# A gated three-branch encoder layer on one core: the last branch's gate blocks four to seven as two Strassen block products

## The chip, the core and the metric

The kernel runs on one core of a Trainium2 chip. TensorE (PE, its weight loads PEld) multiplies, VectorE (DVE), ScalarE (ACT) and GpSimd (POOL) do the elementwise work, SyncE (SP) issues most transfers. The metric is the time of one execution in microseconds (us) of device time. The three runs of the kernel before took 917.25 to 917.41 us, their median is 917.26 us.

## The reference, cut to what matters

One layer for 512 tokens of width 1024. Three branches (A sparse attention, B stick-breaking attention, C attention into memory tokens) are projected up, each multiplied by a sigmoid gate of its own that is computed from the normalised input, and summed; then come an output projection, a norm, and a SwiGLU feed-forward network (FFN).

```
h = rmsnorm(x, g_mix_pre[l])
proj = h @ w_in[l]
aq, ak, av, iq, ik, iw, bq, bk, bv, cq, gate_logits = jnp.split(proj, split_points, axis=-1)
...
ya = dsa_attention(aq, ak, av, iq, ik, iw, rel_bias) @ w_up_a[l]
yb = stick_breaking_attention(bq, bk, bv) @ w_up_b[l]
yc = memory_attention(cq, mk, mv) @ w_up_c[l]
gates = jax.nn.sigmoid((gate_logits + b_gate[l]).astype(jnp.float32)).astype(x.dtype)
gates = gates.reshape(bsz, seq, N_BRANCH, D_MODEL)
merged = gates[:, :, 0] * ya + gates[:, :, 1] * yb + gates[:, :, 2] * yc
x = x + rmsnorm(merged @ w_out[l], g_mix_post[l])
h = rmsnorm(x, g_ffn_pre[l])
gu = h @ w_ffn_in[l]
f = (jax.nn.silu(gu[..., :D_FF]) * gu[..., D_FF:]) @ w_ffn_out[l]
x = x + rmsnorm(f, g_ffn_post[l])
```

## The kernel before

**Precision.** Every float32 operand is split into a high part (a cast to fp32r on ACT) and a low part (the operand less its high part, on DVE). `split` does it, line 74 and line 75. Each block product is then three matmuls, `passes`, lines 85 to 87: high by high, high by low, low by high. So the third matmul of a product is the first that needs the low part of the weights.

**Tiling.** A block is 128 output columns for all 512 tokens. `feat` makes one block over `kc` slices of 128 inputs: a gate block has 8 slices and 24 matmuls of 512 columns, an up-projection block 4 slices and 12 matmuls.

**Merging a branch.** `merge(b, out, wu)` goes over eight blocks j. For each it makes gate block j + 1 (weights from `w_in`, the sum through a sigmoid, L693), the up-projection of block j (`wu` by the branch's output `out`), their product (L709, DVE) and the sum into `acc[j]` (L710, POOL). For branch B, the last one, `acc[j]` is split once more into `mT[j]`, the input of the output projection. Branch B's merge is queued while B's attention runs: its gate blocks 0 and 1 fill gaps of that attention, the rest comes after the attention's end.

**What follows.** `mix_out` (matmuls on L734) multiplies `mT` by `w_out`, adds the rows of `x` (`x1`, tiles `fin`) and norms. `ffn` makes the first three FFN blocks plainly and the other 19 with `seven`: a pair of blocks (gate half and up half) over two token halves is a 2 by 2 block product, and is made as seven products of 12 matmuls of 256 columns each (Strassen's scheme in Winograd's form), 84 matmuls in place of 96 of 256 columns (or 48 of 512). For that the activations have to be combined once (`right_sides`: eight additions on POOL, L828, eight subtractions on DVE, L832, four splits of 1024 columns) and the weights of each pair once (`left_sides`: four subtractions or additions on DVE, L860, three splits of 1024 columns and one of 512).

**Order and buffers.** PE's order is that of the code. On the other engines a scheduler of the compiler sets one fixed order per engine, and each engine works through it in that order. SBUF buffers are tiles of pools: the pool `att` holds the buffers of the attentions, the pool `late` (tags `lraw`, `fin`, `w2`, `s1` to `s3`) is opened after `att` is closed, in the same memory, so its first use waits until the last reader of `att` is done. That reader is the DVE split of branch B's last output (tile `vsum`, read at L75). `wraw`, `wh`, `wl` and `act` are tags of a pool that is open throughout.

Of the kernel before, what the change touches and what calls it, by code (L numbers as in the profile page):

```python
# [11 lines left out]
F32 = mybir.dt.float32  # L12
F32R = mybir.dt.float32r
AF = mybir.ActivationFunctionType
# [3 lines left out]
P = 128  # L18
# [29 lines left out]
class Layer:  # L48
# [212 lines left out]
    def run(self):  # L261
# [4 lines left out]
        with self.tc.manual_schedule(engines={mybir.EngineType.PE}):  # L266
# [412 lines left out]

    def merge(self, b, out, wu):  # L680

        nc, a = self.nc, self.a
        if b == 1:
            self.mT = []
        gates = {}

        def gate(j):
            c = C_G + b * D + j * P
            gw = self.weights(a["w_in"][:, c:c + P], NK, P)
            ps = self.bank()  # L690
            yield from self.feat(ps, gw, self.hT)
            gates[j] = self.sb.tile([P, T], F32, name="gate", tag="gate", bufs=2)
            nc.scalar.activation(gates[j], ps, AF.Sigmoid, bias=self.cols[:, 24 + b * 8 + j:25 + b * 8 + j])  # L693

        yield from gate(0)
        for j in range(NK):
            if j + 1 < NK:
                yield from gate(j + 1)
# [12 lines left out]
            if b == 1:  # L711
                self.mT.append(self.pair("act"))
                self.split(*self.mT[j], self.acc[j])
# [60 lines left out]
    def mix_out(self):  # L774
# [3 lines left out]
        self.x1 = [self.load_rows(a["x"], t, "fin") for t in range(NT)]  # L778
# [38 lines left out]
    def right_sides(self):  # L817

        nc, a, b = self.nc, slice(0, 256), slice(256, 512)
        y = {p: [tuple(x[:, t] for x in self.h2[f + k]) for k in range(4)]  # L820
             for p, f, t in ((1, 0, a), (2, 4, a), (3, 4, b))}
        y |= {p: [] for p in (4, 5, 6, 7)}
        for i in range(2):
            r = [self.big("act", F32).rearrange("p (k t) -> p k t", k=2) for _ in range(2)]
            for f in range(2):
                for k in range(2):
                    hi, lo = self.h2[4 * f + 2 * i + k]
# [12 lines left out]
    def left_sides(self, j):  # L840

        nc = self.nc
        g = self.load(self.a["w_ffn_in"][:, j * P:j * P + P], NK, P, "wraw")[0]
        u = self.load(self.a["w_ffn_in"][:, DFF + j * P:DFF + j * P + P], NK, P, "lraw")[0]
# [30 lines left out]
    def seven(self, j, y, f):  # L875

        nc, x = self.nc, self.left_sides(j)
        px, py, pz = (self.bank()[:, 0:256] for _ in range(3))
        s1, s2, s3 = (self.late.tile([P, 256], F32, name=n, tag=n, bufs=1 + (n == "s3")) for n in ("s1", "s2", "s3"))
        g = self.sb.tile([P, T], F32, name="silu", tag="gate", bufs=2)  # L880
# [6 lines left out]
        nc.vector.tensor_tensor(g[:, 0:256], py, s1, op=OP.add)  # L887
# [102 lines left out]
```

## Time and profile before

| what | value |
|---|---|
| median of 3 runs | 917.26 us |
| the profiled execution's own time | 917.32 us |
| its span, first to last instruction | 915.5 us |
| PE busy | 887.9 us, 97% of the span |
| DVE, ACT, POOL busy | 644.4, 457.6, 122.3 us |
| mean granted clock of TensorE | 0.995 of full speed |

The span is 1.8 us shorter than the execution's time; the difference lies before the first and after the last instruction. A row of a timeline gives start, duration, engine, line, operation and tiles; "x4" means that four instructions are merged in it; brackets give the engine's idle time before it and what ended that. Starts of one engine can lie closer than its durations, since instructions overlap a little.

### The profile page before, as it was taken

Reading aid. Unit: us, or ns where it says so; the run is one execution under the profiler, and the core shown is the slowest. Engines: PE = TensorE matmul, PEld = TensorE weight load, DVE = VectorE, ACT = ScalarE, POOL = GpSimd, SP = SyncE. Lnnn points to the kernel's source line nnn. Section 1 sums busy time; section 2 is a strip of 40 time slices with the busy share of each in tenths; the row PEclk is TensorE's granted clock in tenths of the full one; section 3 lists DMA queues with packets and bytes.
Section 4 is the critical chain, followed back from the end, with each engine's and each line's share of the span. In section 5 each row is a group of like instructions: output and inputs, shape, how many; then the busy total and the mean of one; then the engine's idle time right before and its main releaser. Section 6 shows DMA issues by size and latency. Waiting matters only on the chain.

```text
span 915.5 us, 13446 instructions
## 1 busy us (share of the span) xinstructions
PE 887.9 (97%) x5110; PEld 780.3 (85%) x5110; DVE 644.4 (70%) x1122; ACT 457.6 (50%) x804; POOL 122.3 (13%) x155
## 2 busy tenths in 40 slices
PE   5999999999999999999999999899999999999997
PEld 4889788888888888888788788899999999888885
DVE  7579999963588976777563478688888887932215
ACT  6365575332576666665353355355555555821111
POOL 4000000020032304443212123400000000000000
PEclk9999999999999999999999999899999999999999
DMA  6433543444354433222473524203334334533102
GB/s 213 127 93 116 175 125 93 127 119 112 103 150 127 127 82 92 69 59 58 136 252 107 184 83 125 69 28 112 107 102 116 97 112 131 168 93 100 38 0 92
DMA packets 129541, 101.17 MB, mean 111 GB/s; under 512 B 4652, under 2 KB 115292, under 8 KB 129476
## 3 DMA queue, kind: packets, MB, share of 16 engines
q1 hardware_dynamic: 128884, 99.26, 37.2%
q10 hardware_dynamic: 592, 1.05, 0.3%
q8 instruction: 40, 0.66, 0.3%
q14 instruction: 25, 0.20, 0.1%
HBM read 93.73 MB, written 2.12 MB: 105 GB/s over the span
## 4 chain that ended last, share of the span: by engine, by line
PE 82%; DVE 9%; issue 3%; ACT 2%; DMA 1%; POOL 1%; POOLq 0%; DVEq 0%; SPq 0%; ACTq 0%
PE bank L85 19%; PE bank L86 19%; PE bank L87 19%; PE bank L734 15%; DVE wl L75 3%; PE bank L534 2%; PE bank L549 1%; PE bank L179 1%; PE bank L178 1%; PE bank L209 1%; PE bank L211 1%; PE bank L210 1%; DMA lraw<-in_w_ffn_in_dram 1%; DVE e L621 1%; DVE score L506 1%
## 5 line engine op out<-in xcount | busy, mean ns | idle before, releaser
L75 DVE TENSOR_TENSOR wl<-wraw,wh 128x1024 fp32r<-128x1024 f32 (+1 forms) x112 | 130.6, 1167 | 100.4 <-ACT wh L74 100.1
L74 ACT CAST wh<-wraw 128x1024 fp32r<-128x1024 f32 (+1 forms) x112 | 107.3, 959 | 141.7 <-PE bank L86 79.5
L85 PE MATMUL bank<-h,wh 128*128 128x512 f32 (+1 forms) x376 | 148.8, 396 | 0.0
L87 PE MATMUL bank<-h,wl 128*128 128x512 f32 (+1 forms) x376 | 145.3, 386 | 1.0 <-DVE wl L75 0.9
L86 PE MATMUL bank<-h,wh 128*128 128x512 f32 (+1 forms) x376 | 145.0, 386 | 0.0
L734 PE MATMUL bank<-w,act 128*128 128x512 f32 x360 | 89.0, 393 | 0.0
L87 PEld LDWEIGHTS bank<-h,wl 128*128 128x128 f32 x376 | 70.6, 188 | 15.9 <-DVE wl L75 1.7
L85 PEld LDWEIGHTS bank<-h,wh 128*128 128x128 f32 x376 | 70.9, 189 | 11.7 <-PE bank L341 0.2
L86 PEld LDWEIGHTS bank<-h,wh 128*128 128x128 f32 x376 | 70.8, 188 | 11.4
L734 PEld LDWEIGHTS bank<-w,act 128*128 128x128 f32 x360 | 67.4, 188 | 15.0
L734 PE MATMUL bank<-wh,act 128*128 128x512 f32 x240 | 72.5, 393 | 0.0
L85 PE MATMUL bank<-act,wh 128*128 128x256 f32 (+1 forms) x204 | 69.2, 339 | 0.7 <-DVE s L896 0.7
L86 PE MATMUL bank<-act,wh 128*128 128x256 f32 (+1 forms) x204 | 67.9, 333 | 0.0
L87 PE MATMUL bank<-act,w 128*128 128x256 f32 x228 | 64.1, 281 | 0.0
L85 PE MATMUL bank<-h,w 128*128 128x256 f32 x228 | 64.1, 281 | 0.0
L86 PE MATMUL bank<-h,w 128*128 128x256 f32 x228 | 64.1, 281 | 0.0
L87 PE MATMUL bank<-h,w 128*128 128x256 f32 x228 | 64.1, 281 | 0.0
L85 PE MATMUL bank<-act,w 128*128 128x256 f32 x228 | 64.1, 281 | 0.0
L86 PE MATMUL bank<-act,w 128*128 128x256 f32 x228 | 64.1, 281 | 0.0
L241 POOL TENSOR_TENSOR rs<-ms,mhalf 128x1 f32<-128x1 f32 x18 | 12.1, 674 | 387.7 <-DVE ms L240 384.0
L598 POOL TENSOR_TENSOR p<-toep,score 128x128 f32<-128x128 f32 (+3 forms) x32 | 31.6, 1001 | 199.2 <-DVE score L507 103.0
L734 PEld LDWEIGHTS bank<-wh,act 128*128 128x128 f32 x240 | 45.0, 188 | 9.9
(189 smaller groups left out, 2113.3 us busy)
## 6 DMA issues: line engine op xcount, KB each, us to landing
wraw<-in_w_in_dram SPq DMA_DIRECT2D x64, 512.0 KB, 3.6
lraw<-in_w_ffn_in_dram SPq DMA_DIRECT2D x22, 512.0 KB, 3.9
wraw<-in_w_ffn_in_dram SPq DMA_DIRECT2D x22, 512.0 KB, 3.7
wraw<-in_w_ffn_out_dram SPq DMA_DIRECT2D x11, 512.0 KB, 3.6
lraw<-in_w_ffn_out_dram SPq DMA_DIRECT2D x11, 512.0 KB, 3.5
wraw<-in_w_mem_kv_dram SPq DMA_DIRECT2D x8, 512.0 KB, 3.7
lraw<-in_w_out_dram SPq DMA_DIRECT2D x6, 512.0 KB, 5.5
wraw<-in_w_out_dram SPq DMA_DIRECT2D x6, 512.0 KB, 3.7
```

The lines of the kernel that those rows point to most:

```text
L74: self.nc.scalar.copy(hi, src)
L75: (eng or self.nc.vector).tensor_tensor(lo, src, hi.bitcast(F32), op=OP.subtract)
L85: self.nc.tensor.matmul(out, lhsT=sh, rhs=mh, start=first and i == 0, stop=False, **kw)
L86: self.nc.tensor.matmul(out, lhsT=sh, rhs=ml, start=False, stop=False, **kw)
L87: self.nc.tensor.matmul(out, lhsT=sl, rhs=mh, start=False, stop=last and i == n - 1, **kw)
L178: self.nc.tensor.matmul(out, lhsT=x, rhs=y[:, 0:n], start=True, stop=False)
L179: self.nc.tensor.matmul(out, lhsT=x, rhs=y[:, T:T + n], start=False, stop=True)
L209: self.nc.tensor.matmul(ps, lhsT=ah[:, s], rhs=wh[:, k2], start=st, stop=False)
L241: self.nc.gpsimd.tensor_tensor(r, ms, self.mhalf, op=OP.pow)
L534: self.nc.tensor.transpose(ps[:, c:c + P], p[i][:, j * P:(j + 1) * P], self.ident)
L598: nc.gpsimd.tensor_tensor(s, toep[0][:, 0:n][:, ::-1], self.mask[i], op=OP.add)
L734: self.nc.tensor.matmul(ps[c], lhsT=st_[:, s], rhs=mv_[:, 0, c * 512:(c + 1) * 512], start=f and k == order[0], stop=l and k == order[-1])
```

## The change

Gate blocks 0 to 3 of branch B stay as they are; blocks 4, 5 and 6, 7 become two pairs that `seven` makes. For that `seven` is given its weights, its outputs and what to do with each sum (`glu` is the FFN's form of it), `right_sides` is called a second time, on the input `hT`, and the pool `late` is opened before branch B's merge, not after it. The up-projection's weights of branch B are split into tiles `fin` of the new pool, no longer into `wh` and `wl`. The rows of `x` (`x1`) are loaded some way into `mix_out`, since `fin` has other work before.

```
@@ run
-            self.outB = []
-            self.add(self.merge(1, self.outB, "w_up_b"))
+            self.outB, gates = [], {}
+            self.add(self.gates(1, (0, 1), gates))
             self.branch_b(*b)
-            self.drain()
             att.close()
             self.late = late.enter_context(self.tc.tile_pool(name="late", bufs=1))
+            ys = self.right_sides(self.hT)
+            self.drain()
+            self.add(self.merge_pairs(1, self.outB, "w_up_b", ys, gates))
+            self.drain()
             self.mix_out()
...
+    def merge_pairs(self, b, out, wu, ys, plain):
+        nc, a = self.nc, self.a
+        self.mT = []
+        gates = {}
+        def gate(i):
+            j = 2 * i
+            c = C_G + b * D + j * P
+            gates[i] = g = self.big("fin", F32)
...
+            yield from self.seven(
+                self.left_sides(a["w_in"], c, c + P), ys, g[:, q[0]], g[:, q[1]],
+                lambda: nc.scalar.activation(g[:, 0:512], g[:, 0:512], AF.Sigmoid, bias=bias[0]),
+                second, lambda px: nc.scalar.activation(g[:, q[2]], px, AF.Sigmoid, bias=bias[1]))
+        def up(j):
+            raw, _ = self.load(a[wu][:, j * P:(j + 1) * P], 4, P, "wraw")
+            t = self.big("fin")
+            w = [t[:, c:c + 512].rearrange("p (k c) -> p k c", c=P) for c in (0, 512)]
+            self.split(t[:, 0:512], t[:, 512:1024], raw)
+            y = self.bank()
+            yield from self.feat(y, w, out, kc=4)
...
+        first = 2
+        for j in range(2 * first - 1):
+            if j + 1 not in plain:
+                yield from self.gates(b, (j + 1,), plain)
+            yield from up(j)
+        prev = gate(first)
+        yield from step(prev, 4)
+        yield from up(2 * first - 1)
+        for i in range(first, NK // 2):
+            g = gate(i + 1) if 2 * i + 2 < NK else None
...
@@ mix_out
-        self.x1 = [self.load_rows(a["x"], t, "fin") for t in range(NT)]
+        self.x1 = []
...
+                if not self.x1 and us > 5:
+                    self.x1 = [self.load_rows(a["x"], t, "fin") for t in range(NT)]
@@ right_sides, left_sides, seven
-    def right_sides(self):
+    def right_sides(self, h):
-    def left_sides(self, j):
+    def left_sides(self, w, cg, cu):
-    def seven(self, j, y, f):
+    def seven(self, x, y, g0, g1, first, second, third):
```

PE's order after the attention's end is now: up-projection block 0, gate block 2, up 1, gate 3, up 2, six products of the first pair, up 3, two products of the second pair, the last of the first, up 4, three of the second, up 5, its last two, up 6, up 7.

Three other engines' orders at the attention's end. First DVE, from the last split that the attention itself needs. Before, where `vsum` is the last output of branch B, `act_4643` its low part, `wl_4669` the low part of up block 0's weights, `wl_4693` that of gate block 2's weights and `gate_4616` the product of block 0:

```order
L75 TENSOR_TENSOR wl_4669<-wraw_4666,wh_4668 128x512
L556 TENSOR_TENSOR vsum_4553<-bank_4631,vlow_4640 64x512
L75 TENSOR_TENSOR act_4643<-vsum_4553,act_4643 128x512
L75 TENSOR_TENSOR wl_4693<-wraw_4690,wh_4692 128x1024
L709 TENSOR_TENSOR gate_4616<-bank_4672,gate_4616 128x512
```

After, where `fin_4708` and `fin_4763` hold the weights of up blocks 0 and 1, `w2_4731` those of gate block 2, L895 is the subtraction of `right_sides` and `act_4667`, `act_4671` are low parts of its results:

```order
L75 TENSOR_TENSOR act_4643<-vsum_4553,act_4643 128x512
L895 TENSOR_TENSOR act_4656<-act_4656 128x2x256
L895 TENSOR_TENSOR act_4656<-act_4657,act_4656 128x2x256
L75 TENSOR_TENSOR fin_4708<-wraw_4706,fin_4708 128x512
L895 TENSOR_TENSOR act_4657<-act_4657,act_4656 128x2x256
L75 TENSOR_TENSOR fin_4763<-wraw_4761,fin_4763 128x512
L895 TENSOR_TENSOR act_4657<-act_4657 128x2x256
L75 TENSOR_TENSOR act_4667<-act_4656,act_4666 128x1024
L745 TENSOR_TENSOR gate_4616<-bank_4711,gate_4616 128x512
L75 TENSOR_TENSOR act_4671<-act_4657,act_4670 128x1024
L895 TENSOR_TENSOR act_4674<-act_4674 128x2x256
L75 TENSOR_TENSOR w2_4731<-lraw_4729,w2_4731 128x1024
```

The low part of up block 0's weights moved from ahead of `vsum` to behind two subtractions that follow it, and between `act_4643` and the low part of gate block 2's weights, neighbours before, stand ten instructions.

ACT at the same place, before, where `wh_4692` is the cast of gate block 2's weights and `gate_4664` the sigmoid of gate block 1:

```order
L74 CAST act_4643<-vsum_4553 128x512
L74 CAST wh_4692<-wraw_4690 128x1024
L693 ACTIVATE gate_4664<-bank_4624,cols_96 128x512
L74 CAST wh_4725<-wraw_4723 128x512
L74 CAST act_4687<-act_2069 128x512
```

And after, where `act_4666` and `act_4670` are casts of results of `right_sides`:

```order
L74 CAST act_4643<-vsum_4553 128x512
L74 CAST fin_4708<-wraw_4706 128x512
L74 CAST fin_4763<-wraw_4761 128x512
L74 CAST fin_4818<-wraw_4816 128x512
L74 CAST act_4666<-act_4656 128x1024
L691 ACTIVATE gate_4704<-bank_4624,cols_96 128x512
L74 CAST w2_4731<-lraw_4729 128x1024
L74 CAST act_4670<-act_4657 128x1024
```

The cast of gate block 2's weights has five instructions between itself and `act_4643`, and the second cast of `right_sides` stands behind it.

SP's queue, with the semaphores that each transfer waits for. Before, `wraw_4690` brings gate block 2's weights, and the first load into the pool `late` is `fin_5070`, a row block of `x`:

```order
L95 DMA wraw_4666<-in_w_up_b_dram 128x4x128 [waits DMAHW6_49,DVE_49]
L95 DMA wraw_4690<-in_w_in_dram 128x8x128 [waits DMAHW7_49,DVE_49]
L95 DMA wraw_4723<-in_w_up_b_dram 128x4x128 [waits DMAHW0_49,DVE_49]
L95 DMA wraw_4747<-in_w_in_dram 128x8x128 [waits DMAHW1_49,DVE_49]
L348 DMA fin_5070<-in_x_dram 128x1024 [waits DVE_49,PE_49,Pool_49]
```

After, the first load into `late` is `lraw_4729`, gate block 2's weights, with the same kinds of waits:

```order
L95 DMA wraw_4706<-in_w_up_b_dram 128x4x128 [waits DMAHW6_49,DVE_49]
L95 DMA wraw_4761<-in_w_up_b_dram 128x4x128 [waits DMAHW7_49,DVE_49]
L95 DMA wraw_4816<-in_w_up_b_dram 128x4x128 [waits DMAHW0_49,DVE_49]
L95 DMA lraw_4729<-in_w_in_dram 128x8x128 [waits DVE_49,PE_49,Pool_49]
L95 DMA lraw_4784<-in_w_in_dram 128x8x128
L95 DMA wraw_4840<-in_w_in_dram 128x8x128 [waits DMAHW1_49,DVE_49]
```

The load of gate block 2's weights moved from the second place, in a buffer that is open throughout, to the fourth, in a buffer that waits for the end of the attention.

On POOL the eight additions of `right_sides` (L891) follow the last sum of branch A's merge directly; on all engines the order from the output projection on is as before.

## Rows read from the trace of the kernel before

**Rows 1.** The page: PE's busy time, share and instructions; the clock that was granted in 40 slices; the shares of the chain that ended last.

```profile
PE 887.9 (97%) x5110; PEld 780.3 (85%) x5110; DVE 644.4 (70%) x1122; ACT 457.6 (50%) x804; POOL 122.3 (13%) x155
PEclk9999999999999999999999999899999999999999
PE 82%; DVE 9%; issue 3%; ACT 2%; DMA 1%; POOL 1%; POOLq 0%; DVEq 0%; SPq 0%; ACTq 0%
```

**Rows 2.** Who waited for whom, PE alone: total us, times, longest.

```profile
PE bank L359 <- DVE h L79: 4.4, 2, 2.9
```

**Rows 3.** Busy time of each engine in two stretches: branch B's merge after the attention, and 13 periods of the FFN's pairs. Columns: stretch and its us, then us busy and instructions of PE, PEld, DVE, ACT and POOL, granted clock, DMA share, GB/s.

```profile
452.80:507.20 54.40, 54.40 (x242) 45.06 (x241) 27.82 (x31) 23.93 (x32) 10.91 (x7) 1.00 0.61 193
625.70:754.70 129.00, 129.00 (x1095) 129.00 (x1094) 109.79 (x170) 70.51 (x105) 0.00 (x0) 1.00 0.37 107
```

**Rows 4.** Timeline of PE: the first and third matmul of up block 0, and the first of the output projection.

```profile
452.79 0.39 PE L85 MATMUL bank<-act,wh 128*128 128x512 f32 x1
...
453.25 0.39 PE L87 MATMUL bank<-act,wl 128*128 128x512 f32 x1
...
507.19 0.61 PE L734 MATMUL bank<-wh,act 128*128 128x512 f32 x2
```

**Rows 5.** Timeline of ACT: the SiLU of two FFN pairs, thirteen pairs apart.

```profile
625.69 0.63 ACT L893 ACTIVATE silu<-silu 128x512 f32<-128x512 f32 x1 [1.45 <-DVE silu L892]
...
754.65 0.63 ACT L893 ACTIVATE silu<-silu 128x512 f32<-128x512 f32 x1 [1.45 <-DVE silu L892]
```

**Rows 6.** Timeline of DVE at the attention's end: the low part of branch B's last output, and the low part of gate block 2's weights.

```profile
450.81 0.69 DVE L75 TENSOR_TENSOR act<-vsum,act 128x512 fp32r<-128x512 f32 x1 [0.69 <-ACT act L74]
453.89 1.23 DVE L75 TENSOR_TENSOR wl<-wraw,wh 128x1024 fp32r<-128x1024 f32 x1 [2.39 <-ACT wh L74]
```

**Rows 7.** Groups of ACT's instructions from 440 to 620 us, shapes kept apart: count, us busy, mean ns of one, idle time before.

```profile
L74 ACT CAST wh<-wraw 128x512 fp32r<-128x512 f32 x8 | 5.0, 622 | 8.2 <-PE bank L86 7.2 <-ACT gate L693 1.0
L74 ACT CAST act<-act 128x1024 fp32r<-128x1024 f32 x4 | 4.2, 1055 | 3.2 <-DVE act L832 3.2
L693 ACT ACTIVATE gate<-bank,cols 128x512 f32<-128x512 f32 x8 | 5.5, 683 | 0.0
```

**Rows 8.** Timeline of POOL: the last sum of branch A's merge, and five of the additions of `right_sides` in the FFN.

```profile
439.61 2.27 POOL L710 TENSOR_TENSOR act<-act,gate 128x512 f32<-128x512 f32 x1
...
583.66 6.29 POOL L828 TENSOR_TENSOR act<-h 128x512 f32<-128x512 f32 x5 [0.38 <-DVE h L79]
```

**Rows 9.** Timelines of POOL and DVE where both work from SBUF: first a sum on POOL and a split on DVE in the attention, then DVE through the `right_sides` of the FFN.

```profile
433.00 1.30 POOL L710 TENSOR_TENSOR act<-act,gate 128x512 f32<-128x512 f32 x1 [1.63 <-DVE gate L709]
433.08 2.30 DVE L75 TENSOR_TENSOR wl<-wraw,wh 128x1024 fp32r<-128x1024 f32 x1 [0.16 <-ACT wh L74]
...
588.83 3.93 DVE L832 TENSOR_TENSOR act<-act 128x512 f32<-128x512 f32 x4
592.67 1.22 DVE L75 TENSOR_TENSOR act<-act 128x1024 fp32r<-128x1024 f32 x1
593.81 0.68 DVE L906 TENSOR_TENSOR act<-silu,bank 128x512 f32<-128x512 f32 x1
594.41 1.22 DVE L75 TENSOR_TENSOR act<-act 128x1024 fp32r<-128x1024 f32 x1
595.54 2.94 DVE L832 TENSOR_TENSOR act<-act 128x512 f32<-128x512 f32 x4
598.39 2.48 DVE L75 TENSOR_TENSOR act<-act 128x1024 fp32r<-128x1024 f32 x2
```

**Rows 10.** SP's queue (start and issue time) at the attention's end, and the time from issue to landing of the four loads of `x` into `fin`, 512 KB each.

```profile
440.76 0.37 SPq L95 DMA_DIRECT2D wraw<-in_w_up_b_dram  x1
447.37 0.37 SPq L95 DMA_DIRECT2D wraw<-in_w_in_dram  x1
451.59 1.29 SPq L348 DMA_DIRECT2D fin<-in_x_dram  x3
...
DMA to landing us min/median/max: 3.7/4.2/4.6
```

**Rows 11.** Two pauses of PE at the end of the output projection and the clock. First PE alone in stretches of 1 us (us busy and instructions, granted clock, DMA share, GB/s), then PE's timeline behind the first pause, behind the second one, and two matmuls of 256 columns after it.

```profile
550.00:551.00 1.00, 0.01 (x1) 1.00 0.87 252
...
575.00:576.00 1.00, 0.00 (x0) 0.77 0.00 0
576.00:577.00 1.00, 0.21 (x1) 0.50 0.08 25
...
581.00:582.00 1.00, 1.00 (x7) 0.50 0.01 3
582.00:583.00 1.00, 1.00 (x9) 0.81 0.00 0
...
550.99 0.44 PE L359 MATMUL bank<-ident,act 128*128 128x128 f32 x2 [1.55 <-DVE h L79]
...
576.79 0.69 PE L359 MATMUL bank<-ident,act 128*128 128x128 f32 x2 [2.86 <-DVE h L79]
...
577.91 0.41 PE L85 MATMUL bank<-h,act 128*128 128x256 f32 x1
578.13 0.41 PE L86 MATMUL bank<-h,act 128*128 128x256 f32 x1
```

More of the change, by code (lines that the diff above doesn't have):

```diff
@@ L710, in merge, with second, step @@
                 nc.gpsimd.tensor_tensor(self.acc[j], self.acc[j], g, op=OP.add)
-            if b == 1:
-                self.mT.append(self.pair("act"))
-                self.split(*self.mT[j], self.acc[j])
+    def merge_pairs(self, b, out, wu, ys, plain):
[4 more added lines that the diff above has]
+            j = 2 * i
+            c = C_G + b * D + j * P
+            gates[i] = g = self.big("fin", F32)
+            bias = [self.cols[:, 24 + b * 8 + k:25 + b * 8 + k] for k in (j, j + 1)]
+            q = [slice(256 * k, 256 * k + 256) for k in range(4)]
+            def second(px, s3):
+                nc.vector.tensor_tensor(g[:, q[3]], px, s3, op=OP.add)
+                nc.scalar.activation(g[:, q[3]], g[:, q[3]], AF.Sigmoid, bias=bias[1])
+            yield from self.seven(
[9 more added lines that the diff above has]
+            yield from self.feat(y, w, out, kc=4)
+            g = plain[j] if j in plain else gates[j // 2][:, (j % 2) * 512:(j % 2) * 512 + 512]
+            nc.vector.tensor_tensor(g, y, g, op=OP.mult)
+            nc.gpsimd.tensor_tensor(self.acc[j], self.acc[j], g, op=OP.add)
+            self.mT.append(self.pair("act"))
+            self.split(*self.mT[j], self.acc[j])
+        def step(g, n=1):
+            for _ in range(n):
+                next(g)
+                yield 2.0
+        first = 2
[8 more added lines that the diff above has]
+            g = gate(i + 1) if 2 * i + 2 < NK else None
+            if g:
+                yield from step(g)
+            yield from step(prev)
+            yield from up(2 * i)
+            if g:
+                yield from step(g, 2)
+            yield from up(2 * i + 1)
+            if g:
+                yield from step(g)
+            prev = g
@@ L886, in seven @@
         self.product(py, x[2], y[2], True)
-        nc.vector.tensor_tensor(g[:, 0:256], py, s1, op=OP.add)
+        nc.vector.tensor_tensor(g0, py, s1, op=OP.add)
         self.product(px, x[6], y[6], False)
@@ L891, in seven, with glu, second @@
         self.product(pz, x[3], y[3], False)
-        nc.vector.tensor_tensor(g[:, 256:512], pz, s2, op=OP.add)
-        nc.scalar.activation(g, g, AF.Silu)
+        nc.vector.tensor_tensor(g1, pz, s2, op=OP.add)
+        first()
         yield
         self.product(px, x[7], y[7], False)
-        nc.vector.tensor_tensor(s3, px, s3, op=OP.add)
-        nc.vector.tensor_tensor(f[:, 256:512], g[:, 256:512], s3, op=OP.mult)
+        second(px, s3)
         yield
         self.product(px, x[4], y[4], False)
-        nc.vector.tensor_tensor(f[:, 0:256], g[:, 0:256], px, op=OP.mult)
+        third(px)
         yield
+    def glu(self, j, y, f):
+        nc = self.nc
+        g = self.sb.tile([P, T], F32, name="silu", tag="gate", bufs=2)
+        a, b = slice(0, 256), slice(256, 512)
+        def second(px, s3):
+            nc.vector.tensor_tensor(s3, px, s3, op=OP.add)
+            nc.vector.tensor_tensor(f[:, b], g[:, b], s3, op=OP.mult)
+        return self.seven(self.left_sides(self.a["w_ffn_in"], j * P, DFF + j * P), y, g[:, a], g[:, b],
+                          lambda: nc.scalar.activation(g, g, AF.Silu), second,
+                          lambda px: nc.vector.tensor_tensor(f[:, a], g[:, a], px, op=OP.mult))
     def gated(self, pss, f):
@@ L911, in blocks @@
         for j in js:
-            g = self.seven(j, y, out(j))
+            g = self.glu(j, y, out(j))
             for _ in range(2):
```

33 lines of the change are left out of this document (15 added, 18 removed).

## The prediction, made before the changed kernel ran

> **What bounds the kernel now.** I read the page first: PE is busy for 97% of the span, at full clock but for one slice, and is 82% of the chain that ended last [rows 1]. PE's longest waits behind the start are short [rows 2]. So time is won only by giving PE less to do, and lost wherever PE is made to wait. Then I read the stretch that the change touches. From the first matmul of up-projection block 0 to the first of the output projection PE takes 507.19 - 452.79 = 54.40 us [rows 4], busy throughout at full clock; DVE is busy for 27.8 of it, ACT for 23.9, POOL for 10.9 [rows 3]. PE waits for nothing there: 240 matmuls of 512 columns at 54.40 / 240 = 0.2267 us each. In the FFN, where the same scheme is at work already, PE has no gap either [rows 3], and a pair takes (754.65 - 625.69) / 13 = 9.92 us [rows 5], that is 0.1181 us for each of its 84 matmuls of 256 columns.
>
> **PE's own work.** Two pairs replace 4 x 24 matmuls of 512 columns by 2 x 84 of 256. 144 of the 240 stay: 144 x 0.2267 + 168 x 0.1181 = 32.64 + 19.84 = 52.48 us, against 54.40. The gain is 1.92 us, 0.21% of the whole, and this is all that the change can give: a block product has an eighth fewer columns, but a matmul of 256 columns costs more than half of one of 512. About 0.2% is also what a measurement of this kernel tells from no change.
>
> **What is added.** DVE gets eight subtractions and four splits for the right sides, 8 x 0.7 + 4 x 1.2 = 10.4 us, and about 6 us more for each pair's weights and sums. That lifts DVE from 28 to about 50 us in a stage of some 55. It still fits; the question is where it stands. The order shows it: ten DVE instructions now come between the low part of branch B's output and the low part of gate block 2's weights, which were neighbours. PE has nothing else to do there, since gate block 2 follows up block 0 in its order. I follow the engines from there, in the clock of the trace before; up to this point nothing has moved.
>
> Steps between starts are 593.81 - 592.67 = 1.14 us for a DVE instruction of 1024 columns, 594.41 - 593.81 = 0.60 for 512, (598.39 - 595.54) / 4 = 0.71 for a subtraction of the right sides [rows 9]; a result is there 0.69 (512) or 1.22 (1024) after its start [rows 6, 9]. ACT takes 0.62 and 1.05 for casts, 0.68 for a sigmoid [rows 7]. POOL takes 6.29 / 5 = 1.26 for an addition [rows 8].
>
> 1. POOL is free of branch A's last sum at 439.61 + 2.27 = 441.9 [rows 8]. Eight additions end at 441.9 + 8 x 1.26 = 452.0.
> 2. DVE would start the low part of branch B's output at 450.81 [rows 6]. Where POOL and DVE both work from SBUF, one waits: a split of 1024 columns started 0.08 us after a POOL sum of 1.30 us took 2.30 us, 1.1 more than alone, and the first subtraction of the FFN's right sides waited likewise for the end of POOL's last addition [rows 8, 9]. POOL's eighth addition runs from 450.7 to 452.0. So the low part ends at 452.0 + 0.69 = 452.65 if DVE waits, at 451.5 if not.
> 3. That is the last read of the attention's pool. Before, the first load into `late` was issued at 451.59, 0.09 behind it [rows 6, 10]. Now gate block 2's weights start there (before, at 447.37 [rows 10]), and ACT may first write `fin`: up block 0's cast from 452.7 to 453.3.
> 4. DVE does two subtractions first, then up block 0's low part: 452.6 + 2 x 0.71 = 454.0, ready at 454.7. PE wants it at 453.25 [rows 4]: it stalls for 1.45 us (0.35 without the wait of step 2), and up block 0 ends at 457.0 (455.9).
> 5. DVE: subtraction, split 512, subtraction, split 1024, product of block 0: free at 458.4 (457.3).
> 6. ACT: three casts, a cast of 1024, a sigmoid: free at 456.3. The weights land 4.2 us (3.7 at least) after issue [rows 10], at 456.9. Their cast ends at 457.95, the next one, of the right sides, at 459.0 (457.4).
> 7. DVE's next split needs that last cast, and POOL's sum of block 0 stands in its way from 458.4 to 459.7. Then split, subtraction, and the low part of gate block 2: 459.7 + 1.14 + 0.71 + 1.22 = 462.8. Without any waiting between POOL and DVE and with the fastest landing it is 460.5.
>
> In the undisturbed order PE would take the third matmul of gate block 2 at 452.79 + 14 x 0.2267 = 455.96. The delay is 4.5 to 6.8 us. I take 6.0, nearer to the end with the waits, since the rows show them, but not that a DVE instruction always meets one at these places. It holds both stalls, of about 1 and 5 us, and nothing behind it takes it back, as PE is the bound.
>
> The Trainium skill ("SBUF — State Buffer", section "Who interferes with whom") says that a DVE instruction with two SBUF inputs and a GpSimd instruction that reads SBUF exclude each other for the whole instruction, first come first served. The rows of step 2 agree. By the rule every meeting costs its full wait, the low part comes at 462.8 and the time would be 0.8 us more than I forecast; by the first bound above it would be 1.5 us less.
>
> **The clock.** PE stands from about 456.5 to 462, with two matmuls in between that need the high part alone. Before the second half of the FFN's input it stood similarly: it went on at 576.79 after 2.86 us without work, and the granted clock fell to half within 575 to 576 (0.77 on average there) and came back within 582 to 583 [rows 11]. From 576.8 to 582.4 a matmul of 256 columns took 578.13 - 577.91 = 0.22 us (two start times rounded to 0.01; I use 0.21), so 5.6 us of work lost 5.6 x (1 - 0.118 / 0.21) = 2.4 us. A pause of 1.55 us before 550.99 left the clock at 1.00 [rows 11]. The new pause is the longer kind. No row shows 512 columns at half clock; if they take exactly twice as long the loss is 2.8, and the lower bound is 0. I take 2.4.
>
> **What hides the rest.** Behind 462 DVE has some 16 instructions (low parts of gate block 3, up block 2 and the first pair's first product, the rest of the right sides) and the first pair's subtractions before the second product of that pair, about 13 us, so to 475. PE reaches that product after gate block 2's rest, up 1, gate 3, up 2 and one product: 5.0 + 2.7 + 5.4 + 2.7 + 1.4 = 17 us, at 479. The cover is 4 us and grows with a fallen clock; if it were gone the rest would be added. The second pair comes seven products and an up block later. `x1`, now loaded near 511, is needed when the first half of the output projection is done, some 20 us later, against a landing of 4.6 us at most [rows 10]: nothing. The loads of `w_out` come later than before, but their splits still stand ahead of the last products in DVE's and ACT's orders: nothing. From the output projection on the orders are the old ones.
>
> **The sum.** -1.92 + 6.0 + 2.4 = +6.5 us. On the profiled execution's 917.32 us, which is 0.06 above the median, that makes 923.8; on the median, 923.7 us.
>
> **The rivals.**
> - *The stall comes, the clock holds.* For it: one pause of 1.55 us left it alone, and two matmuls fall into the new pause. Against it: the pause behind them is longer than the one at which it fell. -1.92 + 6.0 = +4.1: 921.3 us. The Trainium skill ("TensorE: Matmul & The Clock Gate", section "HAM oscillation — how this bites in real kernels") warns that pauses between bursts of matmuls send the clock back to half; by that warning the main case holds.
> - *The right sides are hidden, the change is faster.* DVE has idle time while the attention ends (2.39 us before 453.89 alone [rows 6]), and POOL could be done by 452. If the low part of gate block 2 were there by 455.96, PE would never wait and only the 1.92 us remain: 915.3 us. It decides at 457.9: any later, and the gain is eaten. But between the end of the attention's last split, 451.5 at best, and that moment DVE has to do four subtractions for the first half of the right sides and one of the second, three splits of 512 or products and three of 1024: 5 x 0.71 + 3 x 0.60 + 3 x 1.14 = 8.8 us in a fixed order, where 6.4 are there.
> - *The stall is short and eats just the gain*: no difference that can be measured (within 1.8 us), about 918 us, if the low part is there by 459.7. That needs no waiting between POOL and DVE, a clock that holds, and DVE steps 7% shorter than the rows have them (8.2 us for 8.8).
> - *DVE becomes the bound of the whole stage*, with 50 of 55 us: the pairs' own weights come late too. Each of the two would add a microsecond or two: about 926 us. Against it stands the cover of 4 us.
>
> **Numbers.** Chances: stall and fallen clock 0.60, stall with full clock 0.24, later places late as well 0.04, gain hidden 0.06, gain just eaten 0.06. The prediction is the first, 923.7 us. The range takes the first two with their bounds: from -1.92 + 4.5 = +2.6 without the clock, 919.8, a little less for DVE steps that are shorter than I took, to -1.92 + 6.8 + 2.8 = +7.7, 924.9, a little more for a landing later than 4.2 us: 919.4 to 925.8. Faster by over 0.2% 0.06, within 0.2% 0.06, slower by over 0.2% 0.88.
>
> **What the profile after would show.** PE waits twice where up block 0 and gate block 2 begin, the second time for several microseconds, for DVE's low part of tile `w2`; the order on DVE in front of it is full, not idle; the granted clock is 0.5 in a few microseconds behind it; the products of 256 columns then run at 0.118 us without gaps; the output projection starts near 513.5 in place of 507.2. I am wrong if PE has no wait at gate block 2, if the wait is for a transfer and not for DVE, or if the clock stays at 1.00.

## The result and the profile after

The changed kernel takes 929.0 us (median of four runs, 925.6 to 929.6), the kernel before 917.3 us beside it: a ratio of 1.0124 (95% interval 1.0097 to 1.0151). That is 11.8 us slower, where 6.5 were forecast. The profiled execution took 929.6 us, its span is 927.8 us, 12.3 longer than before, and PE is busy for only 3.7 of these 12.3 us more [rows 1]. The page, the line of the engines:

```profile
PE 891.6 (96%) x5182; PEld 784.2 (85%) x5182; DVE 663.7 (72%) x1152; ACT 466.6 (50%) x820; POOL 130.4 (14%) x163
```

PE's waits inside the merge, from 453 to 521 us (us in total, times, longest), the four longest of six; the other two are of 0.2 us:

```profile
PE bank L87 <- DVE w L75: 3.9, 1, 3.9
PE bank L85 <- DVE fin L729: 2.8, 1, 2.8
PE bank L87 <- DVE fin L75: 0.6, 1, 0.6
PE bank L85 <- ACT w L74: 0.4, 1, 0.4
```

Before, PE waited for nothing in this stretch [rows 3]. The first, third and fourth line are the stall that was forecast, at up block 0 (`fin`) and gate block 2 (`w`). The second line was not forecast: L729 is DVE's sum of the seventh product with `s3`, in the last pair. PE's timeline shows both places (start, duration, what ended the idle time):

```profile
454.00 0.39 PE L87 MATMUL bank<-h,wl 128*128 128x512 f32 x1
454.61 0.50 PE L85 MATMUL bank<-act,fin 128*128 128x512 f32 x1 [0.22 <-ACT fin L74]
455.91 0.50 PE L87 MATMUL bank<-act,fin 128*128 128x512 f32 x1 [0.57 <-DVE fin L75]
458.95 0.50 PE L85 MATMUL bank<-h,w 128*128 128x512 f32 x1 [0.45 <-ACT w L74]
463.61 0.79 PE L87 MATMUL bank<-h,w 128*128 128x512 f32 x1 [3.93 <-DVE w L75]
464.20 0.63 PE L85 MATMUL bank<-h,w 128*128 128x512 f32 x1
464.63 0.63 PE L86 MATMUL bank<-h,w 128*128 128x512 f32 x1
...
509.11 0.28 PE L87 MATMUL bank<-act,w 128*128 128x256 f32 x1
512.23 0.39 PE L85 MATMUL bank<-act,wh 128*128 128x256 f32 x1 [2.85 <-DVE fin L729]
512.91 0.41 PE L86 MATMUL bank<-act,wh 128*128 128x256 f32 x1
513.12 0.41 PE L87 MATMUL bank<-act,wh 128*128 128x256 f32 x1
...
520.89 0.62 PE L795 MATMUL bank<-wh,act 128*128 128x512 f32 x2
```

The first row is the last matmul of gate block 1, the last row the first matmul of the output projection. Between their starts lie 66.9 us. Before, the same stretch is one matmul (0.23) and the 54.4 us of [rows 4], 54.6 us. The stage thus holds the whole loss, 12.3 us, and below **the stage** is always this stretch. The granted clock (the number behind POOL's) in the stretch behind each stall:

```profile
463.00:469.00 6.00, 5.39 (x14) 4.29 (x15) 6.00 (x8) 1.41 (x2) 0.00 (x0) 0.56 0.66 175
513.00:517.00 4.00, 4.00 (x17) 3.53 (x17) 2.31 (x3) 2.23 (x3) 0.00 (x0) 0.61 0.92 350
```

It fell to half twice, not once. Matmuls of 512 columns start 464.63 - 464.20 = 0.43 us apart there, those of 256 columns 0.21.

**Where the 12.3 us are**, by starts of matmuls. First stall: 1.33 us at up block 0 (four steps between starts, 0.61 + 0.33 + 0.97 + 0.34, less 4 x 0.23), 4.81 at gate block 2 (0.84 + 0.33 + 4.33, less 3 x 0.23), 2.2 for eleven matmuls at half clock. Second stall: 3.1 us, and 1.6 at half clock. Two short waits in the first pair, for ACT's copies of sums: 0.85. PE's own work: 144 x 0.2333 + 168 x 0.1142 = 52.8 us, a gain of 1.6. Sum: 1.33 + 4.81 + 2.2 + 3.1 + 1.6 + 0.85 - 1.6 = 12.3.

POOL and DVE around the first stall: the eight additions of the right sides, the low part of branch B's output, the second split of the right sides and the low part of gate block 2's weights:

```profile
443.27 10.03 POOL L891 TENSOR_TENSOR act<-h 128x512 f32<-128x512 f32 x8
```

```profile
452.25 1.61 DVE L75 TENSOR_TENSOR act<-vsum,act 128x512 fp32r<-128x512 f32 x1 [0.69 <-ACT act L74]
...
459.87 1.95 DVE L75 TENSOR_TENSOR act<-act 128x1024 fp32r<-128x1024 f32 x1 [0.47 <-ACT act L74]
...
462.35 1.21 DVE L75 TENSOR_TENSOR w<-lraw,w 128x1024 fp32r<-128x1024 f32 x1
```

The ten instructions in between keep DVE busy from 453.78 us on, with one idle time of 0.47 us; PE's wait at gate block 2 ends with the last row.

DVE around the second stall:

```profile
508.66 0.69 DVE L745 TENSOR_TENSOR fin<-bank,fin 128x512 f32<-128x512 f32 x1
510.15 1.69 DVE L75 TENSOR_TENSOR wl<-wraw,wh 128x1024 fp32r<-128x1024 f32 x1 [0.81 <-ACT wh L74]
511.77 0.41 DVE L729 TENSOR_TENSOR fin<-bank,s 128x256 f32<-128x256 f32 x1
```

ACT in the same microseconds:

```profile
509.07 1.05 ACT L74 CAST wh<-wraw 128x1024 fp32r<-128x1024 f32 x1 [0.70 <-DMA wraw<-in_w_out_dram]
```

and POOL:

```profile
509.49 1.27 POOL L746 TENSOR_TENSOR act<-act,fin 128x512 f32<-128x512 f32 x1 [6.11 <-DVE fin L745]
```

The seventh product is done at about 509.4. Its sum, L729, needs nothing else, but stands in DVE's order behind the split of the first rows of `w_out`. That split waits for ACT's cast, which waited for the transfer, and then runs 1.69 us beside POOL's sum. The transfer was issued at 505.39 us, when DVE had freed its buffer. PE's next 12 matmuls (product 4) accumulate on the very bank that L729 reads, so they wait for it.

### The profile page after: what moved, and what is told of

Same layout as the page of the kernel before. It is cut to its first block, busy times and chain, and to the rows that moved or that the text cites. A ratio compares the mean times of both kernels' runs of the same rounds, so it can differ in the third digit from the quotient of the medians.

```text
span 927.8 us, 13650 instructions
## 1 busy us (share of the span) xinstructions
PE 891.6 (96%) x5182; PEld 784.2 (85%) x5182; DVE 663.7 (72%) x1152; ACT 466.6 (50%) x820; POOL 130.4 (14%) x163
## 5 line engine op out<-in xcount | busy, mean ns | idle before, releaser
L75 DVE TENSOR_TENSOR wl<-wraw,wh 128x1024 fp32r<-128x1024 f32 (+1 forms) x98 | 117.1, 1197 | 86.7 <-ACT wh L74 86.3
L74 ACT CAST wh<-wraw 128x1024 fp32r<-128x1024 f32 (+1 forms) x98 | 95.9, 980 | 122.2 <-PE bank L86 60.4
L85 PE MATMUL bank<-h,wh 128*128 128x512 f32 (+1 forms) x328 | 130.1, 397 | 0.0
L87 PE MATMUL bank<-h,wl 128*128 128x512 f32 (+1 forms) x328 | 126.6, 386 | 1.0 <-DVE wl L75 0.9
L86 PE MATMUL bank<-h,wh 128*128 128x512 f32 (+1 forms) x328 | 126.3, 385 | 0.0
L87 PE MATMUL bank<-h,w 128*128 128x256 f32 (+1 forms) x268 | 78.1, 291 | 3.9 <-DVE w L75 3.9
L85 PE MATMUL bank<-h,w 128*128 128x256 f32 (+1 forms) x268 | 78.1, 291 | 0.7 <-ACT w L74 0.4
L86 PE MATMUL bank<-h,w 128*128 128x256 f32 (+1 forms) x268 | 77.7, 290 | 0.0
L87 PEld LDWEIGHTS bank<-h,wl 128*128 128x128 f32 x328 | 61.6, 188 | 14.0 <-DVE wl L75 1.8
L85 PE MATMUL bank<-act,w 128*128 128x256 f32 x252 | 70.8, 281 | 0.1
L87 PE MATMUL bank<-act,w 128*128 128x256 f32 x252 | 70.7, 281 | 0.0
L86 PE MATMUL bank<-act,w 128*128 128x256 f32 x252 | 70.7, 281 | 0.0
L85 PEld LDWEIGHTS bank<-h,wh 128*128 128x128 f32 x328 | 61.9, 189 | 9.8 <-PE bank L344 0.2
L86 PEld LDWEIGHTS bank<-h,wh 128*128 128x128 f32 x328 | 61.8, 188 | 9.6
L85 PE MATMUL bank<-act,wh 128*128 128x256 f32 (+1 forms) x180 | 59.5, 331 | 3.6 <-DVE fin L729 2.8
L86 PE MATMUL bank<-act,wh 128*128 128x256 f32 (+1 forms) x180 | 58.2, 323 | 0.0
L87 PEld LDWEIGHTS bank<-h,w 128*128 128x128 f32 x268 | 50.8, 190 | 5.2 <-DVE w L75 4.4
```

What stands on the lines that cost most here:

```text
L74: self.nc.scalar.copy(hi, src)
L75: (eng or self.nc.vector).tensor_tensor(lo, src, hi.bitcast(F32), op=OP.subtract)
L85: self.nc.tensor.matmul(out, lhsT=sh, rhs=mh, start=first and i == 0, stop=False, **kw)
L86: self.nc.tensor.matmul(out, lhsT=sh, rhs=ml, start=False, stop=False, **kw)
L87: self.nc.tensor.matmul(out, lhsT=sl, rhs=mh, start=False, stop=last and i == n - 1, **kw)
```

## The experiments

Each is timed against the kernel before on its own chip; the medians of before were 916.0 us for the first four runs, 917.0 for the next three and 915.7 for the last one, which was timed once. The stage is read from the profiled execution. Here are all of them; the text on record and what was measured follow.

| kernel | stage, us (before 54.6) | median, us | ratio to before (95%) |
|---|---|---|---|
| changed kernel | 66.9 | 929.0 | 1.0124 (1.0097 to 1.0151) |
| pool early, nothing else | 59.3 | 922.0 | 1.0059 (1.0043 to 1.0075) |
| + right sides, unused | 64.7 | 925.2 | 1.0097 (1.0080 to 1.0113) |
| changed, up block 6 moved | 62.3 | 923.8 | 1.0085 (1.0065 to 1.0104) |
| three moves | 58.9 | 920.8 | 1.0052 (1.0035 to 1.0068) |
| right sides in the attention, additions on DVE | 53.6 | 924.4 | 1.0090 (1.0073 to 1.0106) |
| the same, additions on POOL | 53.6 | 926.1 | 1.0101 (1.0086 to 1.0116) |
| the same, pool early | 57.1 | 930.8 | 1.0154 (1.0136 to 1.0172) |
| kernel before, one tile for both parts | 54.6 | 915.6 (one run) | none |

**1. The pool alone.**

```diff
-            ys = self.right_sides(self.hT)
+            ys = None
...
-        first = 2
-        for j in range(2 * first - 1):
...
+        for j in range(NK):
+            if j + 1 < NK and j + 1 not in plain:
                 yield from self.gates(b, (j + 1,), plain)
             yield from up(j)
...
```

> The changed kernel without its two pairs and without the right sides: gate blocks 2 to 7 are plain blocks again (24 matmuls of 512 columns each), and only the early opening of the FFN buffers stays, with the up-projection weights split into `fin`. Theory (the first stall has two parents, the pool and the right sides): up block 0 waits under half a microsecond; gate block 2's weights are loaded only when the attention's last split is done, land some 4.2 us later, and their low part comes 1.1 + 1.2 us behind that, so PE stands about 2 us at gate block 2; no fall of the clock; no second stall before the output projection. 917.3 + 2.3 = 919.6 us (918.6 to 920.6). Rival A (the pool alone makes the whole stall, the right sides lie beside it): about 6 us of waiting and the clock's 2.3 us, 924 to 926. Rival B (the pool costs nothing, the right sides make all of it): 917.3, no wait at gate block 2.

Measured: a stage of 59.3 us, 4.6 more than before, and 922.0 us, above the range expected. PE's waits in it:

```profile
PE bank L87 <- DVE w L75: 1.6, 1, 1.6
PE bank L85 <- ACT w L74: 0.9, 1, 0.9
```

and the low part of gate block 2's weights on DVE:

```profile
456.35 2.27 DVE L75 TENSOR_TENSOR w<-lraw,w 128x1024 fp32r<-128x1024 f32 x1 [0.17 <-ACT w L74]
```

By starts, the waits cost 3.0 us: the pool makes about half of the first stall, and the clock holds at 1.00. The split began 0.09 us after POOL's sum of up block 0 (456.26, 1.28 us long) and took 2.27 us, where it takes 1.22 alone; PE's wait ends with it. The other 1.6 us of the stage were in nobody's sum: with no wait at all, 24 matmuls of a gate block take 472.31 - 466.71 = 5.60 us, 0.2333 each, not 0.2267. I come back to this with the last experiment.

**2. The right sides, unused.** As in 1, but `ys = self.right_sides(self.hT)` stays.

> The changed kernel with its right sides worked out at their place but used by nothing; all gate blocks are plain blocks of 24 matmuls of 512 columns, so neither the gain of the pairs nor their sums are there. Theory: the first stall is that of the changed kernel, 1.3 us at up block 0 and 4.8 at gate block 2, with some 2.3 us of half clock behind it, and there is no wait for a pair's sum before the output projection: 917.3 + 8.4 = 925.7 us (924.5 to 927). Rival (the pairs' own work on DVE takes part in the first stall): the wait at gate block 2 is shorter than 3 us and the clock holds, 919 to 922. Rival (the second stall comes from the output projection's weights alone and needs no pair): a wait of some 3 us before the output projection here too, 929 to 930.

Measured: a stage of 64.7 us, 10.05 more than before, a ratio of 1.0097. PE's waits in the whole stage:

```profile
PE bank L87 <- DVE w L75: 3.8, 1, 3.8
PE bank L85 <- ACT w L74: 0.6, 1, 0.6
PE bank L87 <- DVE fin L75: 0.6, 1, 0.6
PE bank L85 <- ACT fin L74: 0.2, 1, 0.2
```

and the stretch behind them:

```profile
463.00:469.00 6.00, 5.44 (x14) 4.29 (x15) 5.18 (x7) 1.82 (x2) 0.00 (x0) 0.54 0.65 176
```

These are the first stall's lines of the changed kernel within 0.2 us, with the fall of the clock, and without a single product of a pair. So the first stall is the work of the right sides and the pool together (8.4 us with the clock, and 240 x 0.0066 = 1.6 us of pitch), and the right sides, on top of the pool, make its second half and, with it, the fall. (No run has the right sides at this place without the early pool.) There is no wait before the output projection: the second stall needs the pair.

**3. Up block 6 between product 7 and product 4.**

```diff
-            yield from step(prev)
+            if g:
+                yield from step(prev)
             yield from up(2 * i)
+            if not g:
+                yield from step(prev)
```

> The changed kernel with one move in PE's order: up block 6 stands between the last pair's seventh product and its fourth (which accumulates on the same bank), instead of behind both. Nothing is left out. Theory (the second stall is the wait of the fourth product for DVE's sum of the seventh, which stands behind the split of the first rows of `w_out`): the 12 matmuls of up block 6 take 2.7 us and cover all but some 0.3 us of a wait of 2.85, so the clock does not fall there either: 3.1 + 1.6 - 0.3 = 4.4 us less than the changed kernel's 929.0, so 924.6 us (923.4 to 926), and the first stall stays as it was. Rival (DVE is the bound of the whole stage, so the wait only moves to the next place that needs DVE, up block 7 or the output projection): 928 to 929.5. Rival (the clock falls at a moment of its own, whatever the wait): 926.2.

Measured: a stage of 62.3 us, 4.6 us less than the changed kernel, and 923.8 us. PE's timeline at the place:

```profile
508.75 0.28 PE L87 MATMUL bank<-act,w 128*128 128x256 f32 x1
508.87 0.39 PE L85 MATMUL bank<-act,fin 128*128 128x512 f32 x1
...
511.42 0.40 PE L87 MATMUL bank<-act,fin 128*128 128x512 f32 x1
511.93 0.39 PE L85 MATMUL bank<-act,wh 128*128 128x256 f32 x1
```

and the stretch behind it:

```profile
513.00:517.00 4.00, 4.00 (x22) 3.32 (x21) 3.03 (x4) 1.84 (x3) 1.63 (x1) 1.00 0.93 295
```

Up block 6 covers the wait but for some 0.3 us, and the clock stays at full speed, so neither DVE's load as such nor a clock with a timetable of its own made the second loss. What is left is a stage 7.7 us longer than before, where 6.5 had been forecast for the change. That its 923.8 us look like the 923.7 on record is chance: the kernel before took 916.0 us beside it, not 917.3. Whether an earlier load of `w_out`, or a later place of its split in DVE's order, would also have removed the wait was not tried.

**4. Three moves.** Up block 0 and gate block 2 go back to the old buffers, before the pool is opened; the right sides' subtractions and splits are written after up block 1; up block 6 is moved as in 3.

```diff
+            rs = self.right_sums(self.hT)
+            self.drain()
+            self.mT = []
+            self.add(self.head(gates))
+            self.drain()
             att.close()
...
-        for j in range(2 * first - 1):
+        for j in range(1, 2 * first - 1):
...
+            if j == 1:
+                ys = self.right_sides(self.hT, rs)
```

> The changed kernel with three moves; nothing is left out. Up block 0 and gate block 2 use the old weight buffers and stand before the FFN buffers are opened; the right sides' additions stay where they were, their subtractions and splits are written after up block 1; and up block 6 stands between the last pair's seventh and fourth product. In DVE's order four instructions (three subtractions of the right sides, one split of 512 columns) then stand between the low part of branch B's output and the low part of gate block 2, instead of ten. Theory (each stall is made by what stands ahead on DVE): the wait at up block 0 is gone, that at gate block 2 is 3 x 0.71 + 0.6 us of DVE's work less the idle time that was there, 1 to 2 us, the clock holds, and no wait is left at the last pair: 917.3 - 1.9 + 1.5 + 0.9 of small waits = 917.8 us (915.8 to 919.5). Rival (DVE is too full for the whole stage: what leaves the first stall comes back at the first pair's second product or its left sides): 920 to 924. Rival (the fall of the clock does not need a long wait): half a clock for some microseconds behind gate block 2 here too, 920.

Measured: a stage of 58.9 us and 920.8 us, above the range expected and inside the first rival's; 8 us of the changed kernel's loss are gone, but that rival is seen as well. PE's waits in the stage:

```profile
PE bank L85 <- ACT s L974: 2.4, 1, 2.4
PE bank L85 <- ACT s L979: 0.8, 1, 0.8
PE bank L86 <- DVE act L75: 0.7, 1, 0.7
PE bank L87 <- DVE wl L75: 0.4, 1, 0.4
```

the busy times from 463 to 479 us (DVE's is the third):

```profile
463.00:479.00 16.00, 15.30 (x89) 13.19 (x88) 16.00 (x18) 8.97 (x12) 2.56 (x2) 1.00 0.28 77
```

and ACT's timeline at the place of the longest wait:

```profile
480.92 0.62 ACT L74 CAST act<-act 128x512 fp32r<-128x512 f32 x1 [4.30 <-POOL act L759]
481.44 0.37 ACT L974 COPY s<-bank 128x256 f32<-128x256 f32 x1
```

At gate block 2 PE now waits 0.4 us. But DVE is busy for all 16 of the 16 us behind, and the first pair pays: DVE multiplies up block 2 only at 477.35, POOL adds it from 478.11 to 480.88, ACT's cast of that sum waits 4.30 us for it, and behind the cast stands the copy of a product's sum that PE waits for. The granted clock stays at 1.00 behind that wait of 2.43 us. So the rival that DVE is too full holds here for the part of the stage in which the right sides lie; experiments 5 and 6 take them out and leave no wait there.

**5 to 7. The right sides out of the stage.** They are written ahead of branch B's attention, in 5 with the additions on DVE, in 6 on POOL, both with the other two moves of 4; 7 is as 6 with the pool opened early. The cut shows 5 and 6 against the kernel of 4:

```diff
+            ys = self.right_sides(self.hT)
             self.branch_b(*b)
...
-            rs = self.right_sums(self.hT)
```

> The kernel of the run before (up block 0 and gate block 2 through the old weight buffers and ahead of the opening of the FFN buffers, up block 6 between the last pair's seventh and fourth product), with the right sides now written ahead of branch B's attention, their eight additions on DVE instead of GpSimd. Nothing is left out. In DVE's order all twenty instructions of the right sides then lie between those of the attention, where DVE is busy for some 7 to 8.7 of each 10 us. Theory (in that run DVE was full from 462 to 479 us, since the right sides ran there; taken out of the stage, DVE keeps up and PE waits nowhere in it): the stage takes the 52.5 us of PE's own work and at most 1 us of waits, 917 - 1.5 = 914.5 us against 916.0 before, if the attention takes the 14 us of extra DVE work without a wait. Rival (the attention has no room: DVE's scans set the pace there, and each right-side instruction delays one): 1 to 6 us come back before 452 us, 917 to 921. Rival (the pairs' own left sides alone fill DVE in the stage): waits at the first pair stay, 918 to 920.

> As the run before it in this list, but with the eight additions of the right sides on GpSimd, ahead of branch B's attention. Nothing is left out. GpSimd is busy for 4 of each 10 us there, DVE gets 9 us of right-side work instead of 14. Theory: the stage as there, 52.5 us and at most 1 us of waits, 914.5 us. Rival (GpSimd's additions of 1.26 us lock DVE out and delay the softmax sums that PE waits for): 916 to 920, with waits of PE for GpSimd's `p` or DVE's `pt` in the attention.

> The changed kernel with the right sides written ahead of branch B's attention (additions on GpSimd as in the changed kernel) and up block 6 between the last pair's seventh and fourth product; the FFN buffers open where the changed kernel opens them, with up block 0 and gate block 2 in them. Nothing is left out. Theory (the first stall is the sum of two parents, the pool's 3 us and the right sides' 3): what stays is the wait for gate block 2's weights, as in the run with the pool alone: 0.9 + 1.6 to 2 us, full clock: 916.0 - 1.5 + 3 = 917.5 us (916.5 to 919), and no other wait in the stage. Rival (the two parents overlap, and without the right sides the pool alone still makes 5 us): 920 and more. Rival (attention has no room): waits before 452 us, as in the two runs above.

Measured: in 5 and 6 the stage takes 53.6 us, with no wait of PE that the view lists; it is 1.1 us shorter than before, for the first time. In 7 it takes 57.1 us, and PE's waits there are those of experiment 1. But the attention pays, and the forecast times (914.5, 914.5 and 917.5 us) are missed by 10 to 13 us. PE's waits from 330 to 455 us, first of before, then of 5:

```profile
PE bank L549 <- DVE pt L75: 1.7, 3, 1.1
PE bank L534 <- POOL p L623: 0.7, 1, 0.7
```

```profile
PE bank L540 <- POOL p L629: 6.8, 6, 3.4
PE bank L555 <- DVE pt L75: 2.3, 3, 1.7
```

In 5 the last matmul of gate block 1 starts at 461.06, 8.5 us later than before, with a fall of the clock near 359 us behind the longest of these waits; in 6 at 465.05, 12.5 later, 1.4 of them from the program's start (last section). So the twenty instructions cost 8.5 and 11 us in the attention, more than the 64.7 - 59.3 = 5.4 at their old place. The rival "the attention has no room" is right in all three, but the price is above what it said (8.5 us in 5, where it had 1 to 6). Without the right sides beside it the pool costs here what it cost in experiment 1: 7 less 6 in the stage is 3.5 us, 3.0 of them in the same waits.

**8. One tile for both parts.** In the kernel before, the last branch's up-projection weights lie in one tile, as in `fin`.

```diff
+            if b == 1:
+                raw, _ = self.load(a[wu][:, j * P:(j + 1) * P], 4, P, "wraw")
+                t = self.big("wh")
+                w = [t[:, c:c + 512].rearrange("p (k c) -> p k c", c=P) for c in (0, 512)]
+                self.split(t[:, 0:512], t[:, 512:1024], raw)
...
```

> The kernel before with one edit in the last branch: the up-projection weights' high and low parts stand in the two halves of one tile of 1024 columns (as in the changed kernel), not in two tiles; nothing waits for that and nothing is left out. It is about the pitch of PE's matmuls of 512 columns: 0.2267 us in the kernel before, 0.2333 in every block of the changed kernel whose weights lie in `fin` or `w2`, with waits or without. Theory (the pitch goes with both parts in one tile): 12 matmuls of an up block take 2.80 us, those of a gate block keep 0.2267, and the stage is 8 x 0.08 = 0.6 us longer. Rival (it goes with the place of the FFN buffers, or with what else runs in the stage): 2.72 us for an up block, the stage as before at 54.4 us.

Measured: the theory fell. The stage is as before (452.40 to 507.03), and an up block takes 2.72 us:

```profile
460.79 0.39 PE L85 MATMUL bank<-act,wh 128*128 128x512 f32 x1
...
463.51 0.39 PE L85 MATMUL bank<-h,wh 128*128 128x512 f32 x1
```

In experiment 5, where PE waits for nothing, gate block 2 from the old buffers takes 469.44 - 464.00 = 5.44 us (0.2267), up block 1 from `fin`, just behind, 472.24 - 469.44 = 2.80 (0.2333), and gate block 3 from `w2` 477.84 - 472.24 = 5.60 (0.2333). So the slower pitch needs neither a wait nor a shared tile; in the stage it came with every block of 512 columns whose weights lie in the FFN's buffers. Why is open.

## Why the prediction was wrong

- **The step that failed** is "What hides the rest". It said of the second pair that it "comes seven products and an up block later" and of the splits of `w_out` that they "still stand ahead of the last products in DVE's and ACT's orders: nothing". Both are true, and the second one is the stall. I asked whether those splits come in time for the output projection, whom they serve, and not who stands behind them on DVE: L729, for which PE waits at once, since in the last pair no up block lies between product 7 and product 4. Price: 3.1 us and 1.6 for the clock (experiment 3: 4.6). Without it the stage loses 7.7 us, against the 6.5 of the sum, which is inside the range; the rest is mainly a smaller gain in PE's own work and short waits that the sum did not have.
- **The kernel before showed this wait**, in the FFN's last pair, where nothing lies between the two products either (L896 is the sum of the seventh product there). There too the sum stood in DVE's order behind a split of 1024 columns for later weights, only that this split had not waited for anything. The rows were there to be read, in PE's waits, its timeline and DVE's:

```profile
PE bank L85 <- DVE s L896: 0.7, 1, 0.7
```

```profile
785.84 0.39 PE L85 MATMUL bank<-act,wh 128*128 128x256 f32 x1 [0.71 <-DVE s L896]
```

```profile
784.24 1.22 DVE L75 TENSOR_TENSOR wl<-wraw,wh 128x1024 fp32r<-128x1024 f32 x1
```

- **The first stall** was right in place, cause and size: 1.33 + 4.81 = 6.14 us, forecast 6.0. The wait of step 2 came: the low part of branch B's output took 1.61 us beside POOL's eighth addition, where it takes 0.69 alone [rows 6]. The Trainium skill ("SBUF — State Buffer", "Who interferes with whom") has the later of the two wait for the whole of the other, and the trace agrees here: the addition ends at 453.30, the split 0.56 us later. Experiments 1 and 7 give the pool 3.0 us of the stall's waits; the prediction's working had both parents in one chain and no price for each.
- **The clock** fell as forecast, 2.2 us for 2.4; and again at the second stall, on which nothing had been said. The length of a wait does not decide this alone. Behind waits of 1.6 us (experiment 1) and 2.4 (experiment 4) the granted clock stayed at 1.00; behind one of 2.2 before the second half of the FFN's input in experiment 6 it fell, and behind one of 1.65 near 21 us it fell in five of the ten profiled executions (last section). Experiment 6, PE alone (us busy and instructions, granted clock, DMA share, GB/s):

```profile
589.00:590.00 1.00, 1.00 (x7) 0.50 1.14 343
```

  The Trainium skill ("TensorE: Matmul & The Clock Gate", "HAM oscillation — how this bites in real kernels") describes a kernel in which every wait between bursts of matmuls sends the clock back; in these runs some did and some did not. What decides is open.
- **PE's own work** was forecast 1.92 us shorter. It is 1.6 by the changed kernel's own pitches and 1.1 in a stage without waits (53.6 against 54.6): 108 to 144 matmuls of 512 columns at 0.2333 in place of 0.2267 take back 0.7 to 1.0 us. The pitch of 512 columns had been carried over from other buffers; that of 256, from the FFN, was a little too long (0.1142 in the changed kernel, where the sum had 0.1181).
- **The rivals.** "DVE becomes the bound of the whole stage" had 4 in 100 and named late places that would cost "a microsecond or two". Of the late places one came, with another mechanism than a lack of cover: one instruction in the wrong place in DVE's order. Experiment 3 shows that DVE was not the bound in the changed kernel's later stage; experiment 4 shows it as the bound around the first pair. The right sides could not be hidden at any place that was tried.
- The range ended at 925.8, as it held only the first stall's bounds; a second place was in the chances but not in the range.

None of the kernels beats the one before. The best stage saves 1.1 us, 0.1% of the time, which is less than the half width of every interval in the table (0.15 to 0.27%).

## What to carry to other kernels

When work is put into an engine that runs in order, list for each added or moved instruction not only who waits for it, but who stands behind it on that engine: here a split with nine microseconds of slack (done at 511.84 us, its stage begins at 520.89) held up a sum that had none. An instruction has no slack when it reads a bank on which PE's next product accumulates; put other matmuls between the two products. And a scheme that saves 2 us of a bound engine's time has to find a place for all of its side work: here 20 instructions on DVE and POOL cost 5 to 11 us wherever they were put.

## What the runs showed of the hardware

- In the stage, the pitch of 512-column matmuls is 0.2267 us with weights in the old buffers and 0.2333 with weights in the FFN's, in the same run (experiment 5); a stage of 240 loses 1.6 us by it. The buffer is not the whole of it: in the kernel before, matmuls of gate block 1 from the old buffers start 0.232 us apart from 449.14 to 450.30 us, just behind the attention's last matmuls. The pitch of 256 columns was 0.114 to 0.118, with no cause found.
- At half clock 512 columns took 0.43 us, not twice 0.2267, and 256 columns 0.21.
- Executions of one kernel differ by up to 4.6 us (experiment 4). One part of it seen is a fall of the clock at the program's start that came in some profiled executions (the changed kernel, experiments 2, 3, 6 and 7: 1.4 us later from there on) and not in others (before, 1, 4, 5 and 8). PE's pause just ahead of it is the same in all, 1.64 to 1.66 us. The changed kernel's:

```profile
22.00:24.00 2.00, 2.00 (x11) 2.00 (x11) 1.99 (x5) 0.92 (x2) 0.00 (x0) 0.50 1.02 294
```

and the kernel before:

```profile
22.00:24.00 2.00, 2.00 (x19) 2.00 (x18) 1.93 (x5) 0.67 (x2) 0.00 (x0) 1.00 1.00 264
```

From the start of the output projection to the FFN's pairs, where the pause of [rows 11] lies, the changed kernel is 1.5 us faster than the kernel before: 0.5 ahead of the end of that pause and 1.0 behind it. So the 1.4 us of the start cancel, and the stage's 12.3 us are also the span's.
